# Hybrid recurrence and neighbourhood-attention layer: first attention half in grouped pairs, x a slot earlier, ACT's work on fetched rows in source order, first y rows ahead of w_out

## The chip, the cores and the metric

One core of a Trainium2 chip runs the kernel. The metric is the device time of one execution in microseconds (us); the time of a kernel is the median of its runs. The engines are named as the profile names them: PE (TensorE; PEld is its weight load), DVE (VectorE), ACT (ScalarE), POOL (GpSimd) and SP (SyncE, which here issues the DMAs). Each engine takes its own instructions in order and waits for others by semaphores.

## The reference

One encoder layer on 2048 tokens of width 1024, in float32. The tokens are a grid of 32 rows by 64 columns.

```python
h = layernorm(x) * (1 + scale) + shift            # scale, shift, gate from c @ ada_w + ada_b
q_h, i_h, zf_fw, zf_bw, g_h, q_n, k_n, v_n, g_n = split(h @ w_in)     # nine parts, 1024 columns each
y_hg = hgrn2(q_h, i_h, zf_fw, zf_bw, g_h)         # gated linear recurrence, both directions, 8 heads of 128
o    = neighbourhood_attention(q_n, k_n, v_n, rpb)    # 16 heads of 64
y    = concat([y_hg, o * silu(g_n)]) @ w_out
out  = layernorm(alpha * x + gate * y) * ln_g + ln_b
# attention, for one query at (row r, column c) of one head:
#   keys: 8 grid rows by 16 columns around it, clamped inside the grid
#   s = q . k / 8 + rpb[row offset, column offset];  p = softmax(s);  o = p @ v
```

## The kernel before

[...] The split is a copy on ACT (the high part) and a subtraction on DVE or POOL (the low part). `h`, the normalised and modulated x, is kept as such parts, transposed, in the tiles `h`.

The stages follow one another in time.

1. Startup: half of x is read, normalised and transposed, and the first projections are made.
2. First half of the attention (`first_half`), for tokens 0 to 1023. The 16 heads are eight pairs, one window `w` for each pair. For each pair the attention tile of the first 8 query rows (R = 0) is computed; it has four blocks `j` of 16 columns. What later stages need of q, k, v and g is written to device memory (`nq_d`, `nk_d`, `nv_d`, `ng_d`). In the same windows the other half of x is read, normalised, transposed and split.
3. The recurrence (`hgrn`), both halves.
4. Second half of the attention: for each pair the tiles R = 1, 2, 3, twelve blocks, which need rows of the first half; these are read back ("fetched") into buffers named `bk`, four of them.
5. Output projection with `w_out`, residual, layer norm. `w_out` was split earlier and written to device memory in parts (`wo_d`); `wo_get` reads parts back into the places where `h` was, and `y_raw` reads rows of the branches' outputs (`yq`), which `y_split` splits.

In stages 2 and 4 `weave` lays the attention of one pair (`natten_woven`, a generator) over a dense stream of matmuls: the projections of the next pair (`first_stream`, `natten_stream`) or the output projection (`out_stream`). Whenever `natten_woven` yields a number, the stream is advanced to the same share of its total as the yielded numbers have of `steps`. So PE's order is written out by hand, by the order of the source. In one pair the attention's own work is: `scores` (matmuls against the keys' high parts `KA`, `KB`, L1001, and against the low parts `KL`, L1005), `softmax` on DVE and ACT (L1018 to L1028), `turned` (transposes of the shares on PE, L1050, copied out of the accumulator banks by DVE, L1054, and ACT, L1056), and `sums` (shares times V, L1069). The list `pipe` holds the blocks whose sums are still due. In the second half, blocks come in pairs: both blocks' scores stand together. In the first half, each block stands alone: scores of one block, sums of an older one, a stretch of the stream, transposes, another stretch.

Between these steps stand tasks (`tasks(i)`): loads of V and of bias tables, key copies, splits of Q, gates, and in the first half the 32 slots of `first_half`, four for each pair, with the steps of the second half of x (`rows`, `stats`, `scale`, `piece`) and loads for the gate of the residual (`gate_load`, `gate_sum`).

The order on the other engines is made by a scheduler that simulates the kernel. It lets an instruction move ahead of others; work in `tc.high_priority(offset=PRI)`, such as the softmax and the copies out of banks, goes first. `pinned` (`tc.keep_in_program_order`) puts an instruction behind the one traced just before it on its engine. Accumulators are PSUM banks, eight in all: two for the projections (`pj`), and six that are shared out anew in each stage. In the first half these are two for scores (`sc`), two for transposes (`pt`, those of x included), two for the sums (`po`); in the second half four for scores and transposes together (`sp`), and two for sums.

Names in the prediction: L953 is the exponential of a gate; L923 and L924 copy the two high parts of Q, L938 those of keys; L774 and L800 are splits of weights into high and low parts, of which L801 is the low part; L178 is a step of the statistics of x; L273 is the V projection and L279 its copy out of the bank; L260 the other projections; L910 fetches rows, L1390 is the load in `wo_get`, L1394 the load in `y_raw`, L1420 the copy in `y_split`, L1428 the first matmul of the output projection; L473 and L484 belong to the recurrence.

Of the kernel before, what the change touches and what calls it, by code (L numbers as in the profile page):

```python
# [19 lines left out]
P = 128  # L20
# [17 lines left out]
def body(ctx: ExitStack, tc: tile.TileContext, t):  # L38
# [179 lines left out]
    def h_piece(xs, k, hi, lo, early=False):  # L218
        pt = ps("pt")
# [680 lines left out]
    class Prep:  # L900
# [16 lines left out]

        def q(self, R):
# [4 lines left out]
            act.activation(av[0:64], rv[0:64], AF.Copy)  # L923
            act.activation(bv[64:128], rv[64:128], AF.Copy)  # L924
# [4 lines left out]
        def k(self, i):  # L929
            a, b, src, off = KPIECE[self.half][i]  # L930
            n = (b - a) * GW
            raw = (self.bk[src] if src in self.bk else self.raws["k"][src])[:, off:off + n]
# [3 lines left out]
            for z, x, y in (("KA", top, bot), ("KB", bot, top)):  # L936
                z = keys[z]
                act.activation(z[x, o], raw[x], AF.Copy)  # L938
# [11 lines left out]
        def gate(self, R):  # L950
            raw = self.src("g", R)
            sg = tl("sg")
            act.activation(sg, raw, AF.Exp, scale=-1.0)  # L953
# [141 lines left out]
    def natten_woven(st, nxt, pipe, extra=None, finish=False):  # L1095
# [8 lines left out]
        def tasks(i):  # L1104
            for f, *a in now.get(i, []) + later.get(i, []) + extra.get(i, []):
                f(*a)

        if st.half == 0:
            for i, (R, j) in enumerate(n.order):
                pipe.append([n, R, j, n.scores(R, [j])[0]()])  # L1110
                if len(pipe) > 2:
                    m, r, c, pts = pipe.pop(0)
                    m.sums(r, c, pts)
                yield 1
                turn(pipe, 2)
                yield 1
                tasks(i)
            if finish:
                m, r, c, pts = pipe.pop(0)
                m.sums(r, c, pts)  # L1120
                yield 1
                turn(pipe, 1)
                yield 1
                m, r, c, pts = pipe.pop(0)
                m.sums(r, c, pts)
            return
# [27 lines left out]
    SPS = {"sc": 2, "pt": 2, "po": 2}  # L1154
# [92 lines left out]
    def first_half(raws, feed):  # L1247
# [8 lines left out]
        for j in (0, 1):  # L1256
            st.table("top", j)
# [25 lines left out]
        for m in range(8):  # L1283
            slots[2 + m].append((gate_load, m))
            slots[4 + m].append((gate_sum, m))
        slots[5].append((lower_bounds,))
        for g, i in ((0, 11), (1, 22)):
            slots[i].append((rows, g))
            slots[i + 1].append((stats, g))
            slots[i + 2 - g].append((scale, g, 0))  # L1290
            slots[i + 3 - g].append((scale, g, 1))
            for k in range(KT):
                slots[i + 3 - g + k].append((piece, g, k))
        for u in range(2, 8):
            slots[4 * u - 6].append((bias_pair, u))
        for w in range(8):
# [4 lines left out]
            else:  # L1301
                nxt, dense, total, steps = None, hgrn_dense(0, 0, feed=feed), HTOT, 10
# [45 lines left out]
    with tc.manual_schedule(engines={mybir.EngineType.PE}):  # L1348
        with psum_phase("st", SPS), phase("st", SB_, SMS), tc.manual_schedule(engines={getattr(mybir.EngineType, e) for e in ("PE", "SP", "Activation", "DVE")}):
# [245 lines left out]
```

## Time and profile before

| | |
|---|---|
| time, median of 3 runs | 2683.83 us (2682.41 to 2684.12) |
| the profiled execution | 2687.64 us, span 2685.8 us |
| mean granted clock of PE | 0.989 |
| PE, PEld busy | 2585.7 us (96%), 2154.1 us (80%) |
| DVE, ACT, POOL busy | 66%, 53%, 4% |
| DMA | 313.25 MB, 117 GB/s on average |

The span runs from the first to the last instruction of the profiled execution. Busy time is summed over the instructions of an engine. An idle stretch of an engine is put down to the instruction that released it: "PE pj L273 <- ACT vt L279" is a matmul of line 273, into tile `pj`, that waited for an ACT instruction of line 279 which wrote `vt`. In rows of the timeline, the first number is the start in us from the beginning of the span, the second the duration, `x2` the number of instructions that were joined, and brackets hold the wait before it. In rows of the table of stretches stand the stretch, its length, then for PE, PEld, DVE, ACT and POOL the busy time with the number of instructions, then the granted clock of PE (1.00 is full speed), the busy share of the DMA engines, and GB/s.

### The profile page before, as it was taken

How to read it: one execution, taken by the hardware profiler on the slowest of the kernel's cores; microseconds unless marked ns; L12 is line 12 of the kernel's file. 1: busy time of each engine (PE TensorE's matmuls, PEld its weight loads, DVE VectorE, ACT ScalarE, POOL GpSimd, SP SyncE). 2: the span in 40 equal slices, each digit the busy share in tenths (PEclk: the TensorE clock that was granted, in tenths of full speed). 3: DMA queues.
4: the chain of work that ended last, by engine and by line, in shares of the span. 5: the costliest groups of instructions: out<-in, count | busy, mean ns of one | idle time of the engine just before them, and what ended most of it. 6: DMA issues, size and time to landing. Idle time of an engine off the chain costs nothing.

```text
span 2685.8 us, 46076 instructions
## 1 busy us (share of the span) xinstructions
PE 2585.7 (96%) x17328; PEld 2154.1 (80%) x17328; DVE 1764.1 (66%) x4351; ACT 1423.0 (53%) x2808; POOL 106.6 (4%) x143
## 2 busy tenths in 40 slices
PE   4999999999999999999999999979999998999998
PEld 3888888878888888888888888878877776788887
DVE  5445445478777778877777877545787776548443
ACT  4534444366666666666666666444666665331110
POOL 0000000000000000000000000000000000032221
PEclk8999999999999999999999999999999999999999
DMA  6566454312222237312221122353444446544331
GB/s 235 158 179 161 127 164 150 112 64 91 79 83 87 80 103 242 108 58 75 76 78 61 62 73 83 99 161 98 123 135 130 132 133 175 159 150 134 98 94 55
DMA packets 235777, 313.25 MB, mean 117 GB/s; under 512 B 29480, under 2 KB 118312, under 8 KB 235433
## 3 DMA queue, kind: packets, MB, share of 16 engines
q1 hardware_dynamic: 235553, 310.30, 37.6%
q8 instruction: 136, 2.23, 0.4%
q14 instruction: 88, 0.72, 0.1%
HBM read 226.63 MB, written 75.37 MB: 112 GB/s over the span
## 4 chain that ended last, share of the span: by engine, by line
PE 67%; DMA 4%; DVE 4%; ACT 2%; issue 1%; SPq 1%; DVEq 0%; ACTq 0%
PE pj L260 37%; PE ps L1430 4%; PE ps L1428 4%; PE ps L1429 4%; PE ps L1069 2%; PE ps L1050 2%; PE ps L473 2%; PE pj L273 2%; PE ps L465 1%; PE ps L1001 1%; PE ps L540 1%; PE ps L564 1%; PE ps L566 1%; PE ps L512 1%; DMA bias<-tint 1%; PE ps L1005 1%
## 5 line engine op out<-in xcount | busy, mean ns | idle before, releaser
L260 PE MATMUL pj<-h,wh 128*128 128x512 f32 x4016 | 1283.3, 400 | 12.3 <-ACT h L225 5.9
L260 PEld LDWEIGHTS pj<-h,wh 128*128 128x128 f32 x4016 | 730.0, 189 | 170.6 <-issue 14.8
L260 PE MATMUL pj<-h,wl 128*128 128x512 f32 x2008 | 787.2, 392 | 0.0
L260 PEld LDWEIGHTS pj<-h,wl 128*128 128x128 f32 x2008 | 377.8, 188 | 82.9 <-DVE wl L801 0.4
L273 PE MATMUL pj<-wh,h 128*128 128x256 f32 x1024 | 195.2, 288 | 13.1 <-ACT vt L279 12.8
L1023 ACT ACTIVATE pbuf<-pbuf,mx 128x480 f32<-128x480 f32 (+2 forms) x224 | 143.1, 640 | 121.8 <-DVE mx L1018 120.4
L1018 DVE CUSTOM_DVE_ANT_1 pbuf<-ps,bias 128x480 f32<-128x480 f32 (+2 forms) x224 | 125.7, 590 | 106.2 <-PE ps L1005 91.2
L273 PEld LDWEIGHTS pj<-wh,h 128*128 128x128 f32 x1024 | 163.7, 193 | 16.8 <-ACT vt L279 14.1
L251 DVE TENSOR_TENSOR wl<-wr,wh 128x512 fp32r<-128x512 f32 x192 | 131.7, 686 | 45.6 <-ACT wh L250 44.8
L250 ACT ACTIVATE wh<-wr 128x512 fp32r<-128x512 f32 x192 | 120.2, 626 | 72.9 <-PE pj L260 60.0
L1056 ACT ACTIVATE pt<-ps 128x512 f32<-128x512 f32 (+1 forms) x128 | 69.1, 540 | 148.1 <-PE ps L1050 147.9
L273 PE MATMUL pj<-wl,h 128*128 128x256 f32 x512 | 145.8, 285 | 0.0
L1054 DVE COPY pt<-ps 128x512 f32<-128x512 f32 (+1 forms) x128 | 79.4, 620 | 87.8 <-PE ps L1050 86.9
L1050 PE MATMUL ps<-ident,pbuf 128*128 128x128 f32 x776 | 106.2, 274 | 12.2 <-ACT pt L1056 12.2
L459 DVE TENSOR_TENSOR de<-e,de 128x512 f32<-128x512 f32 x64 | 44.3, 692 | 108.5 <-ACT de L458 108.5
L1050 PEld LDWEIGHTS ps<-ident,pbuf 128*128 128x128 f32 x776 | 92.2, 140 | 28.4 <-ACT pt L1056 13.0
L1404 ACT ACTIVATE yh<-yr 128x512 fp32r<-128x512 f32 x52 | 32.7, 629 | 134.0 <-PE ps L1429 115.4
L1477 DVE TENSOR_TENSOR vt<-ps,gt 128x512 f32<-128x512 f32 x24 | 16.5, 692 | 128.5 <-PE ps L1430 128.5
L1069 PE MATMUL ps<-pt,V 128*64 128x128 f32 x1408 | 100.3, 278 | 0.5 <-DMA V<-nv 0.5
L273 PEld LDWEIGHTS pj<-wl,h 128*128 128x128 f32 x512 | 99.1, 194 | 0.8 <-issue 0.5
L1028 DVE TENSOR_SCALAR pbuf<-pbuf,mx 128x480 f32<-128x480 f32 (+2 forms) x224 | 96.0, 437 | 5.4
L748 ACT ACTIVATE e<-pj 128x512 f32<-128x512 f32 x100 | 59.3, 594 | 74.2 <-PE pj L260 68.6
(271 smaller groups left out, 4722.7 us busy)
## 6 DMA issues: line engine op xcount, KB each, us to landing
wr<-in_w_in SPq DMA_DIRECT2D x276, 256.0 KB
V<-nv SPq DMA_DIRECT2D x256, 64.0 KB
yr<-yq SPq DMA_DIRECT2D x64, 256.0 KB
bias<-tint SPq DMA_DIRECT2D x24, 480.0 KB
x<-in_x SPq DMA_DIRECT2D x32, 256.0 KB
ada<-in_ada_w SPq DMA_DIRECT2D x16, 512.0 KB
wr<-in_w_v SPq DMA_DIRECT2D x32, 256.0 KB
nv<-vt SPq DMA_DIRECT2D x32, 256.0 KB
```

The source lines that it names most:

```text
L250: act.activation(hi, raw, AF.Copy)
L251: dve.tensor_tensor(lo, raw, hi, op=ALU.subtract)
L260: pe.matmul(pz, a, b, start=(k == 0 and n == 0), stop=(k == KT - 1 and n == 2))
L273: pe.matmul(pzs[tp][:, i * 256:(i + 1) * 256], a, b, start=(k == 0 and n == 0 and i == 0), stop=(k == KT - 1 and n == 2), skip_group_check ...
L1018: return dve.tensor_tensor_reduce(s[:, 0:nk].rearrange("p (r c) -> p r c", c=32), sc[:, 0:nk].rearrange("p (r c) -> p r c", c=32), bt[:, 0 ...
L1023: act.activation(s[:, 0:nk], s[:, 0:nk], AF.Exp, scale=-1.0, bias=mx[:, 0:1], accum_out=mx[:, 1:2])
L1028: dve.tensor_scalar(s[:, 0:nk], s[:, 0:nk], mx[:, 2:3], 1.0, op0=ALU.mult, op1=ALU.mult)
L1050: pe.transpose(ptp[:, c * P:(c + 1) * P], s[:, c * P:(c + 1) * P], ident)
L1069: pe.matmul(self.po[R][hs_, j * P:(j + 1) * P], self.st.V[c0 + c][:, j * P + hh * 64:j * P + hh * 64 + 64], pts[hh][:, c * P:(c + 1) * P], ...
L1428: pe.matmul(pz, yh[:, kk], wh, start=first, stop=False)
L1429: pe.matmul(pz, yh[:, kk], wl, start=False, stop=False)
L1430: pe.matmul(pz, yl[:, kk], wh, start=False, stop=last)
```

## The change

1. First half, `natten_woven`: the four blocks of a pair come as two groups of two. The sums that are due stand first, then the scores of both blocks of the group, then both softmaxes; after a stretch of the stream the transposes of both blocks, then another stretch. The tasks of a pair keep their slots; within a slot the `extra` ones come first, in the second half too. The banks are shared out as in the second half (four for scores and transposes), with one for the sums and one for the transposes of x. Three top bias tables are loaded ahead of the first window instead of two, and the last window is counted as 9 steps instead of 10.
2. `first_half`: the loads for the residual's gate and all steps of x stand one slot earlier (the second group's scaling and pieces keep theirs).
3. `Prep`: the ACT instructions that read fetched rows (Q of R = 1, key pieces 0 and 1, gate of R = 1) are pinned to the order of the source.
4. The first four y rows are loaded at slots 2 and 3 of the second half's pair 6, pinned, into buffers of `vt`; before, they were loaded at slots 10 and 11 into weight buffers. For the second column of `w_out`, the first two parts are read ahead of pair 7, and the others one slot earlier than before.

```diff
 def h_piece(xs, k, hi, lo, early=False):
-    pt = ps("pt")
+    pt = ps("hx")
...
 class Prep:
+    def pin(self, raw):
+        return pinned if any(raw is z for z in self.bk.values()) else lambda ins: ins
...  # in q, k and gate:
-        act.activation(av[0:64], rv[0:64], AF.Copy)
-        act.activation(bv[64:128], rv[64:128], AF.Copy)
+        pin = self.pin(raw)
+        pin(act.activation(av[0:64], rv[0:64], AF.Copy))
+        pin(act.activation(bv[64:128], rv[64:128], AF.Copy))
...
-            act.activation(z[x, o], raw[x], AF.Copy)
+            pin(act.activation(z[x, o], raw[x], AF.Copy))
...
-        act.activation(sg, raw, AF.Exp, scale=-1.0)
+        self.pin(raw)(act.activation(sg, raw, AF.Exp, scale=-1.0))
...
 def natten_woven(st, nxt, pipe, extra=None, finish=False):
     def tasks(i):
-        for f, *a in now.get(i, []) + later.get(i, []) + extra.get(i, []):
+        for f, *a in extra.get(i, []) + now.get(i, []) + later.get(i, []):
             f(*a)
     if st.half == 0:
-        for i, (R, j) in enumerate(n.order):
-            pipe.append([n, R, j, n.scores(R, [j])[0]()])
-            if len(pipe) > 2:
-                m, r, c, pts = pipe.pop(0)
-                m.sums(r, c, pts)
-            yield 1
-            turn(pipe, 2)
-            yield 1
-            tasks(i)
-        if finish:
-            ...
+        for i in (0, 2):
+            sums(pipe, 0)
+            for j, soft in zip((i, i + 1), n.scores(0, (i, i + 1))):
+                pipe.append([n, 0, j, soft()])
+            yield 2
+            tasks(i)
+            turn(pipe, 2)
+            turn(pipe, 1)
+            yield 2
+            tasks(i + 1)
+        if finish:
+            sums(pipe, 0)
+            yield 1
         return
...
-    SPS = {"sc": 2, "pt": 2, "po": 2}
+    SPS = ({"sc": 2, "pt": 2, "po": 2}, {"hx": "pt"})
+    NPS0 = ({"sp": 4, "po": 1, "hx": 1}, {"sc": "sp", "pt": "sp"})
...  # first_half
-        for j in (0, 1):
+        for j in (0, 1, 3):
             st.table("top", j)
...
         for m in range(8):
-            slots[2 + m].append((gate_load, m))
-            slots[4 + m].append((gate_sum, m))
+            slots[1 + m].append((gate_load, m))
+            slots[3 + m].append((gate_sum, m))
-        for g, i in ((0, 11), (1, 22)):
+        for g, i in ((0, 10), (1, 21)):
             slots[i].append((rows, g))
             slots[i + 1].append((stats, g))
-            slots[i + 2 - g].append((scale, g, 0))
-            slots[i + 3 - g].append((scale, g, 1))
+            slots[i + 2].append((scale, g, 0))
+            slots[i + 3].append((scale, g, 1))
             for k in range(KT):
-                slots[i + 3 - g + k].append((piece, g, k))
+                slots[i + 3 + k].append((piece, g, k))
...  # the second half's windows
                 if u == 6:
-                    extra = {6: [(wo_get, 0, 0, 1)], 7: [(wo_get, 0, 2)], 8: [(wo_get, 0, 3)], 9: [(wo_get, 0, 4, 5)], 10: [(y_early, 0), (wo_get, 0, 6)], 11: [(y_early, 1), (wo_get, 0, 7)]}
+                    extra = {6: [(wo_get, 0, 0, 1)], 7: [(wo_get, 0, 2)], 8: [(wo_get, 0, 3)], 9: [(wo_get, 0, 4, 5)], 10: [(wo_get, 0, 6)], 11: [(wo_get, 0, 7)]}
+                    for i in (2, 3):
+                        extra[i] = [(lambda tt: y_early(tt, alloc=lambda: tl("wr")), i - 2)]
             else:
                 y_split(0, 1)
                 dense, total = out_stream(list(range(NE))), NE * 16 * KUS
-                extra = {i: [(wo_get, 1, 2 * i, 2 * i + 1)] for i in range(4)}
+                wo_get(1, 0, 1)
+                extra = {i: [(wo_get, 1, 2 * i + 2, 2 * i + 3)] for i in range(3)}
```

More of the change, by code (lines that the diff above doesn't have):

```diff
@@ L931, in k @@
             n = (b - a) * GW
-            raw = (self.bk[src] if src in self.bk else self.raws["k"][src])[:, off:off + n]
+            raw = self.bk[src] if src in self.bk else self.raws["k"][src]
+            pin, raw = self.pin(raw), raw[:, off:off + n]
             o = slice(a * GW, b * GW)
@@ L1104, in tasks @@
         def tasks(i):
-            for f, *a in now.get(i, []) + later.get(i, []) + extra.get(i, []):
+            for f, *a in extra.get(i, []) + now.get(i, []) + later.get(i, []):
                 f(*a)
         if st.half == 0:
-            for i, (R, j) in enumerate(n.order):
-                pipe.append([n, R, j, n.scores(R, [j])[0]()])
-                if len(pipe) > 2:
-                    m, r, c, pts = pipe.pop(0)
-                    m.sums(r, c, pts)
-                yield 1
-                turn(pipe, 2)
-                yield 1
-                tasks(i)
-            if finish:
-                m, r, c, pts = pipe.pop(0)
-                m.sums(r, c, pts)
-                yield 1
[L1122 to L1125, printed above, removed]
+            for i in (0, 2):
[10 more added lines that the diff above has]
+                sums(pipe, 0)
+                yield 1
             return
@@ L1301, in first_half @@
             else:
-                nxt, dense, total, steps = None, hgrn_dense(0, 0, feed=feed), HTOT, 10
+                nxt, dense, total, steps = None, hgrn_dense(0, 0, feed=feed), HTOT, 9
             r = weave(natten_woven(st, nxt, pipe, extra, w == 7), dense, total, steps)[1]
@@ L1348, in body @@
     with tc.manual_schedule(engines={mybir.EngineType.PE}):
-        with psum_phase("st", SPS), phase("st", SB_, SMS), tc.manual_schedule(engines={getattr(mybir.EngineType, e) for e in ("PE", "SP", "Activation", "DVE")}):
+        with psum_phase("st", *SPS), phase("st", SB_, SMS), tc.manual_schedule(engines={getattr(mybir.EngineType, e) for e in ("PE", "SP", "Activation", "DVE")}):
             raws, feed = startup()
-        with psum_phase("n0", SPS), phase("n0", NB0, SM0):
+        with psum_phase("n0", *NPS0), phase("n0", NB0, SM0):
             natten_init(4, 0)
@@ L1390, in wo_get, with y_raw @@
                 pinned(dma(wo[k, n][s].bitcast(F32), wo_d[2 * k + n][s]))
-    def y_raw(tt, q):
-        raw = wp.tile([P, 512], F32, tag="wraw", name=nm("yr"), bufs=WR)
-        dma(raw.rearrange("p (a b) -> p a b", b=P), yq[q][:, :, tt * P:(tt + 1) * P])
+    def y_raw(tt, q, alloc=None):
+        raw = alloc() if alloc else wp.tile([P, 512], F32, tag="wraw", name=nm("yr"), bufs=WR)
+        (pinned if alloc else lambda i: i)(dma(raw.rearrange("p (a b) -> p a b", b=P), yq[q][:, :, tt * P:(tt + 1) * P]))
         return raw
@@ L1408, in body, with y_early @@
     yraws, yhl = {}, {}
-    def y_early(*tts):
+    def y_early(*tts, alloc=None):
         for tt in tts:
             for q in range(2):
-                yraws[tt, q] = y_raw(tt, q)
+                yraws[tt, q] = y_raw(tt, q, alloc)
     def y_split(*tts):
```

## The prediction

> **What bounds the kernel now.** I read the page's busy line first, then the list of waits for PE alone, then the granted clock in stretches, and last the timelines of ACT and SP ahead of the long waits.
>
> ```profile
> span 2685.8 us, 46076 instructions
> PE 2585.7 (96%) x17328; PEld 2154.1 (80%) x17328; DVE 1764.1 (66%) x4351; ACT 1423.0 (53%) x2808; POOL 106.6 (4%) x143
> ```
>
> PE is busy for all but 100 us of the span. So only two things can pay: PE's idle time, and PE's own time for the same matmuls. The waits of PE, longest first after the one at startup:
>
> ```profile
> PE pj L273 <- ACT vt L279: 12.8, 2, 11.9
> PE ps L1050 <- ACT pt L1056: 12.2, 2, 11.2
> PE pj L260 <- ACT h L225: 5.9, 7, 1.4
> PE ps L1001 <- DVE pt L1054: 5.2, 5, 1.0
> PE ps L331 <- DVE rh L326: 4.6, 8, 1.4
> PE ps L473 <- DVE Sf L484: 4.0, 2, 2.8
> PE pj L1428 <- DMA wo<-wod: 3.6, 1, 3.6
> PE pj L260 <- ACT wh L774: 2.9, 1, 2.9
> PE pj L260 <- ACT wh L800: 2.1, 1, 2.1
> ```
>
> Columns: total, times, longest. Two single waits, 11.9 and 11.2 us, stand out. I call them A and B, the 3.6 C, the 2.9 D, the 2.1 E, the 2.8 F. They cost more than themselves, because the clock falls after them (PEclk is the last column but two):
>
> ```profile
> 355.00:394.00 39.00, 39.00 (x270) 33.93 (x268) 15.97 (x41) 15.81 (x34) 0.76 (x3) 1.00 0.52 165
> 296.04:299.45 3.41, 3.41 (x12) 2.24 (x12) 0.53 (x2) 0.00 (x0) 0.00 (x0) 0.50 0.71 235
> 1808.74:1814.96 6.22, 6.22 (x29) 6.22 (x30) 4.32 (x11) 4.29 (x9) 0.00 (x0) 0.50 0.73 233
> 1836.00:2272.00 436.00, 427.12 (x3035) 345.48 (x3033) 335.83 (x961) 283.13 (x633) 6.28 (x20) 1.00 0.50 131
> 2280.51:2286.00 5.49, 5.49 (x19) 3.86 (x19) 5.14 (x16) 4.39 (x10) 0.00 (x0) 0.50 0.45 145
> 2313.31:2316.72 3.41, 3.38 (x9) 1.99 (x9) 0.00 (x0) 0.00 (x0) 0.00 (x0) 0.50 1.05 381
> ```
>
> PE works at 0.50 for 6.22 us after A, 5.49 after B, 3.41 after C and 3.41 after E; half of each stretch is lost.
>
> **Wait A, and the pins.** ACT takes its instructions in order, and the scheduler had put the next pair's gate (L953) far ahead of its place. Rows of the timeline, ACT's and SP's (start, duration, instruction, wait before it):
>
> ```profile
> 1805.78 0.63 ACT L953 ACTIVATE sg<-bk 128x512 f32<-128x512 f32 x1 [18.24 <-DMA bk<-ng]
> ...
> 1808.10 1.07 ACT L279 ACTIVATE vt<-pj 128x512 f32<-128x512 f32 x2
> 1801.93 0.32 SPq L910 DMA_DIRECT2D bk<-ng  x1
> ```
>
> ACT stands for 18.24 us on a row whose load SP issued only at 1801.93. Behind it wait the two copies of `vt` that free PE's accumulators. The pin holds L953 (and Q, K from fetched rows, L923, L924, L938) behind the ACT instruction traced just before it; the gate's place is slot 11, the end of the pair. The same instructions run, none is added. Gain: 11.9 + 6.22/2 = 15.0 us. What is late next: V rows and key copies, which SP issues until 1805, but the blocks that need them come after several more microseconds of projections; I take 0 and keep half of A and B together, 14.5 us, as the rival below.
>
> The four fetched rows' buffers come free later by it, and SP's next fetch with them: 0, since the next fetch is issued when the pair after begins, behind that gate. The pin has another price. Before, the gate, Q and K of the next pair floated into free places. Now the gate's work falls on each pair's end, where five waits of 1.0 (L1001 on DVE's L1054) show DVE to be tight. Queued there are ACT's other copies and DVE's; the gate brings DVE one clamp and one product. The nearest row is that wait itself: between 0 and another 1.0 at seven ends. I take 0.5 each, 3.5 us, because softmax and bank copies have priority over the gate. Below nothing it can hardly be: those waits could vanish if ACT or DVE have less in that place, 5 us at most.
>
> **Wait B, and the first y rows.** Timeline again:
>
> ```profile
> 2264.29 0.63 ACT L924 ACTIVATE Q<-e 64x512 fp32r<-64x512 f32 x1
> 2277.73 0.63 ACT L1420 ACTIVATE yh<-yr 128x512 fp32r<-128x512 f32 x1 [12.81 <-DMA yr<-yq]
> ...
> 2279.98 0.47 ACT L1056 ACTIVATE pt<-ps 128x384 f32<-128x384 f32 x1
> 2267.76 2.01 SPq L1390 DMA_DIRECT2D wo<-wod  x4
> 2269.87 3.76 SPq L1394 DMA_DIRECT2D yr<-yq  x2
> ```
>
> Again ACT's queue has a split of a fetched row (L1420) at its head, for 12.81 us, and the bank copy L1056 behind it. The row's load was issued at 2269.87, behind w_out's parts, which wait on PE for the buffers of h. The change issues the four loads at slots 2 and 3 of pair 6, some 40 us ahead, into buffers of `vt` that nothing uses then. L1420 finds its rows landed. Gain: 11.2 + 5.49/2 = 13.9 us. On SP the four loads move past w_out's parts and into the stream of V rows and weights; four of them took 2.69 us (row below), and SP's own issue is not what PE waits for in pair 6, so 0, at most those 2.7 us.
>
> ```profile
> 2303.13 2.69 SPq L1394 DMA_DIRECT2D yr<-yq  x4
> 2305.91 5.49 SPq L1390 DMA_DIRECT2D wo<-wod  x8
> ```
>
> **Wait C, and w_out's second column.** Its last eight loads were issued from 2305.91 on, just ahead of PE's wait. Now two parts come before pair 7 begins, the others one slot earlier each, and ahead of the key copies of their slot (extra work first). Sixteen issues move past four key copies and eight V loads on SP; these are needed a third of the pair later. Gain 3.6 + 3.41/2 = 5.3 us. But with B gone PE comes to this place 14 us sooner, while SP has the same issues to make: between 5.3 gained and 5.3 lost. I take 5.3 with 1.0 given back, since half of each load's lead is won by order alone.
>
> **First half: grouped pairs.** One step of one block, in PE's timeline:
>
> ```profile
> 251.75 0.32 PE L1001 MATMUL ps<-KA,q 128*128 128x352 f32 x1
> 251.91 0.32 PE L1001 MATMUL ps<-KB,q 128*128 128x352 f32 x1
> 252.17 0.43 PE L1005 MATMUL ps<-KL,q 64*128 64x352 f32 x2
> 252.53 0.88 PE L1069 MATMUL ps<-pt,V 128*64 128x128 f32 x12
> 253.33 0.73 PE L260 MATMUL pj<-h,wh 128*128 128x512 f32 x2
> ```
>
> Starts to starts: 1.58 us, 3.16 for two blocks. The second half already groups:
>
> ```profile
> 1926.92 0.62 PE L1005 MATMUL ps<-KL,Q 64*128 64x384 f32 x4
> 1927.47 0.88 PE L1069 MATMUL ps<-pt,V 128*64 128x128 f32 x12
> ...
> 1929.37 0.73 PE L260 MATMUL pj<-h,wh 128*128 128x512 f32 x2
> ```
>
> Four KL take 0.55 there at 384 columns, so 0.55 x 352/384 = 0.50 here, against 2 x 0.36. All 32 sums take 1.90, and 12 alone 0.80; so 12 more cost (1.90 - 0.80) x 12/20 = 0.66, and 24 take 1.46 against 1.60. KA and KB: 3 x 0.16 + 0.26 = 0.74 against 0.84. Entering the sums straight from projections adds a change of shape, 0.26 - 0.16 = 0.10. Together 0.10 + 1.46 + 0.74 + 0.50 = 2.80; saved 0.36 per group, and 16 groups (two for each of eight pairs) give 5.8 us. The same counts of instructions run on every engine. [...]
>
> The softmax of two blocks must now end within a quarter of a pair. A pair without V took 39 us with 15.97 us of DVE and 15.81 of ACT (first row of the clock stretches): even all DVE work of half a pair, 8 us, is less than the quarter's 9.75. I take 3.0 us for small new waits in 16 groups, bounds 0 and the slower rival. The transposes of x get a bank of their own (one, spaced a slot), the sums one instead of two, read half a pair before its reuse: 0. The third table loaded at the start: 0, behind the V projection of the first pair; the next pair's second table has half a pair of lead instead of three quarters, some 20 us: 0.
>
> **x a slot earlier.** Wait E:
>
> ```profile
> 286.69 0.21 ACT L178 ACTIVATE l<-v 128x4 f32<-128x4 f32 x1 [7.24 <-DVE v L176]
> ```
>
> ACT stands 7.24 us for the statistics of x, then has the scalings, powers and weight splits (L800) all at once, when the V projections end. A slot earlier, eight loads, eight statistics and eight scalings come before and during those projections, where PE asks ACT for little. Gain 2.1 + 3.41/2 = 3.8; if the statistics now meet a softmax, 0, or the same lost. I take 3.8. F lies behind DVE's backlog as the recurrence starts; the sums that end the half come a ninth of the window sooner, so it may go (2.8, and by the stretch after E another 1.7 for the clock); I take 0. D stays: the split L774 keeps its place.
>
> **The sum.** 15.0 + 13.9 + 5.3 + 5.8 + 3.8 = 43.8 gained; 3.5 + 1.0 + 3.0 = 7.5 given back, some of it doubtful; forecast 36.3 less. The profiled execution took 2687.64 us (span 2685.8), 3.8 above the median of 2683.83, so 2651.3 there and 2647.5 as a median. [...]
>
> **Rivals.** (1) Forecast, 0.52. (2) A and B only shrink: ACT or SP has another fetched thing at its head, and half of 28.9 is given back: 2662. For it: SP issues without pause before A and around B. Against: ACT did nothing else for 18 and 13 us. 0.22. (3) Nothing is given back and F goes too: 2683.8 - 43.8 - 4.5 = 2635.5; 0.15. (4) Slower: in each first-half group PE waits for banks or for the second block's softmax, all four score banks being taken at once. It decides from 36.3/16 = 2.3 us a group, with the clock 1.7 lower behind each: at 1.0 + 1.7 it is even worse than the gain, 36.3 - 43 = 7 us slower, 2690.6. The second half runs on such a pool of four: five waits of 1.0 there and no stretch at half clock from 1836 to 2272 (1.00 in the row), so 0.07. [...] (5) No change within 0.2%, 5.4 us, about what a measurement here can tell: the gains of the second half lost again at pair ends, 0.04.
>
> Cases 1 to 3 hold 0.89. The range is 2633 to 2666: from case 3 with a little more to case 2 with C lost. The likeliest case alone: 2640 to 2655.
>
> **What would show it.** Right: L953 no longer among ACT's waits on DMA; L1420 without a wait; PE's L273 and L1050 waits under 2 us each; no half-clock stretch near those places; two KL groups and 24 sums together in the first half. Wrong: L1001 or L1050 waiting on DVE in the first half, pair ends with more than 1.0, or PE waiting for w_out longer than 3.6.

## The result and the profile after

The changed kernel takes 2670.41 us (median of 5 runs, 2663.61 to 2675.12) against 2683.83 before: ratio 0.9949, 95% interval 0.9932 to 0.9966, 13.4 us less. Forecast were 36.3 less and a range from 2633 to 2666. It is faster, by little more than a third of the forecast.

The profiled execution took 2663.61 us, 6.8 below its median, and that of before 3.8 above its own; the two profiles differ by 24.0 us, the medians by 13.4. So places are read from the profiles here, and sizes of whole parts from ratios (0.001 is 2.7 us; the ratio 0.9949 makes 13.7). Line numbers move by the change: after it L1006 and L1010 are the scores, L1023 is the first step of the softmax, L1074 the sums, L1055 the transposes, L1059 and L1061 their copies; L718, L725 and L726 load bias tables, L944 copies keys from one half of the partitions to the other, L952 loads V; L1392 is the load in `wo_get`, L1396 that in `y_raw`, L1422 the copy in `y_split`, L1430 the first matmul of the output projection.

Where the 24.0 lie, from the starts of three rows in each PE timeline: the first scores of the first half's last pair, of the second half, and of pair 6's last group. Before (L1001), then after (L1006, the same instruction):

```profile
486.62 0.41 PE L1001 MATMUL ps<-KA,q 128*128 128x352 f32 x1
1781.92 0.39 PE L1001 MATMUL ps<-KA,Q 128*128 128x480 f32 x1
2260.99 0.34 PE L1001 MATMUL ps<-KA,Q 128*128 128x384 f32 x1
```

```profile
480.18 0.43 PE L1006 MATMUL ps<-KA,q 128*128 128x352 f32 x1
1771.03 0.39 PE L1006 MATMUL ps<-KA,Q 128*128 128x480 f32 x1
2230.16 0.34 PE L1006 MATMUL ps<-KA,Q 128*128 128x384 f32 x1
```

Gained are 6.4 us up to the first half's last pair, 4.5 to the second half, 19.9 in pairs 0 to 6. From pair 6's last scores to the end of the span it is 2685.8 - 2261.0 = 424.8 before and 2661.8 - 2230.2 = 431.6 after: 6.8 lost, where the forecast had 18.2 gained. I call this stretch the tail. The gain ahead of it, 30.8 us in all, is the upper end of what the runs show: in the seven profiles of kernels that differ from the changed one in the tail alone (after_again, y_late, half_wo, late_half, no_table, no_col and table_spread, below), pair 6's last scores start at 2232.8 to 2241.2, which is 20 to 28 us ahead of before. So most of the difference between 24.0 and 13.4 lies ahead of the tail. PE's waits after the change:

```profile
PE ps L1006 <- issue: 13.6, 1, 13.6
...
PE pj L1430 <- DMA wo<-wod: 4.6, 1, 4.6
PE pj L1430 <- ACT yh L1422: 3.6, 2, 2.4
PE pj L260 <- ACT wh L774: 2.9, 1, 2.9
PE pj L273 <- ACT vt L279: 2.5, 1, 2.5
...
PE ps L1055 <- DVE pt L1059: 1.5, 1, 1.5
```

A (11.9 before L273) is down to 2.5, B (11.2 before the transposes) is gone, and so are E and the five waits of 1.04 at pair ends. C is gone too. C was a wait on the second column of `w_out`: in PE's timeline it stands before the 21st matmul of L1428, and the first column, eight parts for two token tiles, has the first 16. The 4.6 us after the change stand before the eighth matmul of L1430 (at 2273.06), so they are a wait on the last part of the first column. In B's place stands a wait of 13.6 before pair 7's scores. What the new wait is, the timelines of SP, DVE and PE and SP's own list of waits tell:

```profile
2229.41 0.72 SPq L725 DMA_DIRECT2D bias<-tedge  x1
2230.18 0.51 SPq L726 DMA_DIRECT2D bias<-tint  x1
...
2231.77 0.60 SPq L718 DMA_DIRECT2D bias<-tint  x1
2232.41 5.03 SPq L1392 DMA_DIRECT2D wo<-wod  x4
2242.36 3.65 SPq L1396 DMA_DIRECT2D yr<-yq  x3
2247.75 0.52 SPq L944 DMA_DIRECT2D KA<-KA  x1
...
2249.65 1.32 SPq L944 DMA_DIRECT2D KA<-KA  x2
...
2242.43 0.56 DVE L1023 CUSTOM_DVE_ANT_1 pbuf<-ps,bias 128x384 f32<-128x384 f32 x1 [5.09 <-DMA wo<-wod]
...
2253.44 0.74 PE L1006 MATMUL ps<-KA,Q 128*128 128x480 f32 x1 [13.59 <-issue]
...
SPq L1396 <- DMA bias<-tint: 4.8, 1, 4.8
```

PE could go on at 2239.9. The keys' copies (L944), which the scores need, were issued only from 2247.75 on, behind w_out's parts and y rows of the third and fourth tile (L1396, not pinned; the scheduler brought them forward into the weight buffers that the first rows no longer use). SP was not busy with issuing all that time: its list of waits says that it stood for 4.8 us, ahead of these y rows, until a bias table had landed. DVE's last softmax of pair 6 went on in the same moment. The profile names a part of `w_out` as what released it, but this instruction reads a bias table and none of `w_out`, so the table is the likelier one.

The granted clock falls here too: it is 0.57 from 2244 to 2260 (0.67 from the wait's end, 2253.44, on) and 0.74 from 2260 to 2280.

### The profile page after: what moved, and what is told of

Read it like the earlier page. It is cut to its first block, busy times and chain, and to the rows that moved or that the text cites. A ratio compares the mean times of both kernels' runs of the same rounds, so it can differ in the third digit from the quotient of the medians.

```text
span 2661.8 us, 46149 instructions
## 1 busy us (share of the span) xinstructions
PE 2574.7 (97%) x17328; PEld 2151.1 (81%) x17328; DVE 1761.2 (66%) x4351; ACT 1417.6 (53%) x2808; POOL 105.3 (4%) x143
## 4 chain that ended last, share of the span: by engine, by line
PE 87%; DVE 5%; DMA 4%; ACT 3%; issue 1%; SPq 0%; DVEq 0%; ACTq 0%
PE pj L260 49%; PE pj L273 5%; PE ps L1431 4%; PE ps L1430 4%; PE ps L1432 4%; PE ps L1074 3%; PE ps L1055 3%; PE ps L473 2%; PE ps L1006 2%; PE ps L465 1%; PE ps L1010 1%; PE ps L540 1%; PE ps L564 1%; PE ps L566 1%; PE ps L512 1%; DMA V<-nv 1%
## 5 line engine op out<-in xcount | busy, mean ns | idle before, releaser
L1023 DVE CUSTOM_DVE_ANT_1 pbuf<-ps,bias 128x480 f32<-128x480 f32 (+2 forms) x224 | 125.5, 589 | 117.5 <-PE ps L1010 95.7
L273 PE MATMUL pj<-wh,h 128*128 128x256 f32 x1024 | 193.6, 287 | 2.8 <-ACT vt L279 2.5
L273 PEld LDWEIGHTS pj<-wh,h 128*128 128x128 f32 x1024 | 162.7, 193 | 6.1 <-ACT vt L279 3.4
L251 DVE TENSOR_TENSOR wl<-wr,wh 128x512 fp32r<-128x512 f32 x192 | 131.5, 685 | 45.7 <-ACT wh L250 44.4
L273 PE MATMUL pj<-wl,h 128*128 128x256 f32 x512 | 145.5, 284 | 0.3 <-DVE wl L801 0.3
L1059 DVE COPY pt<-ps 128x512 f32<-128x512 f32 (+1 forms) x128 | 79.0, 618 | 58.9 <-PE ps L1055 58.1
L1061 ACT ACTIVATE pt<-ps 128x512 f32<-128x512 f32 (+1 forms) x128 | 68.9, 539 | 91.1 <-PE ps L1055 89.9
L1055 PE MATMUL ps<-ident,pbuf 128*128 128x128 f32 x776 | 103.8, 274 | 1.5 <-DVE pt L1059 1.5
L1055 PEld LDWEIGHTS ps<-ident,pbuf 128*128 128x128 f32 x776 | 91.2, 141 | 15.5 <-DVE pt L1059 1.7
L273 PEld LDWEIGHTS pj<-wl,h 128*128 128x128 f32 x512 | 98.8, 193 | 1.3 <-DVE wl L801 0.5
L801 DVE TENSOR_TENSOR wl<-wr,wh 128x512 fp32r<-128x512 f32 x68 | 46.8, 690 | 78.7 <-ACT wh L800 68.2
```

The source lines that it names most:

```text
L251: dve.tensor_tensor(lo, raw, hi, op=ALU.subtract)
L273: pe.matmul(pzs[tp][:, i * 256:(i + 1) * 256], a, b, start=(k == 0 and n == 0 and i == 0), stop=(k == KT - 1 and n == 2), skip_group_check ...
L1023: return dve.tensor_tensor_reduce(s[:, 0:nk].rearrange("p (r c) -> p r c", c=32), sc[:, 0:nk].rearrange("p (r c) -> p r c", c=32), bt[:, 0 ...
L1055: pe.transpose(ptp[:, c * P:(c + 1) * P], s[:, c * P:(c + 1) * P], ident)
```

## The experiments

Ratios are to the kernel before, run beside each kernel. "Wait" is PE's wait before pair 7's scores; "tail" is read as above. The intervals are 0.001 to 0.0017 to either side, so the difference of two rows is uncertain by some 0.002, 5 us. Waits and tails come from one profile each.

| run | ratio (95%) | wait, us | tail, us |
|---|---|---|---|
| kernel before | 1 | none | 424.8 |
| changed kernel | 0.9949 (0.9932 to 0.9966) | 13.6 | 431.6 |
| after_again | 0.9949 (0.9935 to 0.9962) | 15.2 | 432.5 |
| no_pin | 0.9984 (0.9975 to 0.9993) | 1.5 | 427.4 |
| no_group | 0.9983 (0.9973 to 0.9992) | 16.0 | 434.8 |
| no_slot | 0.9979 (0.9970 to 0.9988) | 16.8 | 435.1 |
| no_y | 0.9929 (0.9916 to 0.9941) | 11.7 | 430.6 |
| gate_pin | 0.9946 (0.9931 to 0.9961) | 1.9 | 429.6 |
| before_gate | 0.9964 (0.9951 to 0.9976) | 0.2 | 424.1 |
| y_pinned | 1.0761 (1.0746 to 1.0776) | 10.2 | - |
| y_late | 0.9937 (0.9925 to 0.9949) | 12.5 | 427.5 |
| ord_back | 0.9970 (0.9959 to 0.9982) | 10.2 | 429.8 |
| wo_early | 0.9929 (0.9917 to 0.9941) | 8.3 | 421.9 |
| half_wo | 0.9914 (0.9900 to 0.9928) | 11.1 | 423.1 |
| late_half | 0.9914 (0.9901 to 0.9927) | 8.2 | 419.8 |
| no_table | 0.9915 (0.9901 to 0.9929) | 11.2 | 426.7 |
| mix | 0.9922 (0.9910 to 0.9935) | 5.3 | 423.2 |
| mix_d | 0.9909 (0.9896 to 0.9922) | 9.0 | 420.8 |
| no_col | 0.9900 (0.9885 to 0.9915) | 0.4 | 413.7 |
| table_spread | 0.9937 (0.9923 to 0.9951) | 5.8 | 422.9 |

y_pinned has another last stage, so its tail is not compared. wo_early has a new wait of 3.3 us just ahead of its tail.

**The changed kernel again.**

> The changed kernel once more, to have it beside the next three on one chip and to see how far its own waits move from run to run. Expected: ratio 0.995, the wait before L1006 between 11 and 17 us as in the runs that keep the pins on the keys.

The wait moves by 1.6 us and the time by nothing.

### Each part undone

**no_pin**

```diff
-            return pinned if any(raw is z for z in self.bk.values()) else lambda ins: ins
+            return lambda ins: ins
```

> The changed kernel without the pins on ACT's work on fetched rows. Theory: the pins took away wait A and also the five waits of 1.04 us at the ends of the second half's pairs (both are absent after the change), so both come back: a wait of PE on L279 of about 12 us with the clock at half behind it, 15 us, and 5 us at pair ends; about 2690 us against 2670.4 of the changed kernel. Rival: the place of the gate depended on the old order of the first half and does not return; then no wait over 3 us on L279 and 2670 to 2675.

PE's waits:

```profile
PE pj L1430 <- DMA wo<-wod: 13.0, 2, 8.6
PE pj L273 <- ACT vt L279: 12.2, 3, 10.8
...
PE ps L1006 <- DVE pt L1059: 6.1, 6, 1.0
```

A is back with 10.8 and the waits at pair ends with six of 1.0, as the theory said; the pins are worth 0.0035, 9.4 us, about half of what it had. The wait before pair 7's scores goes, but the last two parts of w_out's first column are waited for 13.0 in its place: the tail shortens by 4 us only.

**no_group** (banks, tables and steps of before too)

```diff
-            for i in (0, 2):   # two blocks' scores together
+            for i, (R, j) in enumerate(n.order):   # one block
```

> The changed kernel with the first half's blocks one by one again (banks, tables and steps of before too). Theory: grouping gained about 6 us of PE's own time (the stretch from the first scores to those of the first half's last pair took 373.5 us before and 367.5 after), so 2676; the wait before L473 where the recurrence starts (2.8 us before, 1.6 after) returns with its half clock, another 3: 2679. Rival: the 6 us come from x's new slot and the wait that went with it (E, 3.8); then grouping is worth 2 us, 2672.

```profile
PE ps L473 <- DVE Sf L484: 2.8, 1, 2.8
```

Ratio 0.9983: grouping is worth 9.1 us with F, which comes back at the recurrence's start as the theory said (after the change 1.6 us are left in that place, behind ACT).

**no_slot**

```diff
-            slots[1 + m].append((gate_load, m))
+            slots[2 + m].append((gate_load, m))
...  # the same for gate_sum and the first group of x; rows and stats of the second
```

> The changed kernel with x and the residual's gate back in their old slots of the first half. Theory: with grouped scores, wait E (2.1 us before L260 on L800, with 3.4 us at half clock) was gone by the slots, so it returns: 4 us slower than the changed kernel, ratio to before about 0.996 to 0.997. Rival: grouping took E away by itself, and the slots are worth nothing: ratio 0.995 as the changed kernel's.

The slots are worth 8.1 us by the ratios, twice the theory's, though with the uncertainty above not surely more than it. E is not at its old place; two others of its kind are there, in PE's timeline:

```profile
169.12 0.38 PE L273 MATMUL pj<-wh,h 128*128 128x256 f32 x1 [1.66 <-ACT wh L800]
...
455.28 0.33 PE L221 MATMUL ps<-ident,x 128*128 128x128 f32 x1 [2.25 <-ACT x L214]
```

**no_y**

```diff
-                    extra = {6: ..., 10: [(wo_get, 0, 6)], 11: [(wo_get, 0, 7)]}
-                    for i in (2, 3): extra[i] = [(lambda tt: y_early(tt, alloc=...), i - 2)]
+                    extra = {6: ..., 10: [(y_early, 0), (wo_get, 0, 6)], 11: [(y_early, 1), (wo_get, 0, 7)]}
...  # pair 7's w_out slots, and the order within a slot of the second half, as before
```

> The changed kernel with the first y rows and w_out's parts back in their old slots and buffers. From the first scores of pair 7's predecessor's last group to the end the profile of before took 415.8 us, that of the changed kernel 422.6, with a new wait of 13.6 us before L1006. Theory: part 4 itself put that wait there, and lost about what wait B had cost: undone, wait B (L1055 on L1061, 11 us) returns and the 13.6 goes; the time is the same or up to 7 us less, 2663 to 2671. Rival: the 13.6 us come from the pins or from the earlier end of the windows before; then undoing part 4 adds its forecast gain, 14 to 19 us, and the time is about 2685.

The time is as the theory said, the reason not: B does not come back, and the 13.6 does not go. With the pins, PE stands before pair 7's scores (11.7) ahead of the place where B was. A wait of 3.5 on the second column is back, as C was. So part 4 as a whole is worth nothing here: without it the ratio is lower by 0.0020, and the intervals only just overlap. The forecast had 18.2 us for it.

**ord_back**, the order within a slot alone:

```diff
-            for f, *a in extra.get(i, []) + now.get(i, []) + later.get(i, []):
+            for f, *a in (now + later + extra if st.half else extra + now + later):   # of slot i
```

> The changed kernel with the order of tasks within a slot of the second half as before (the extra tasks last), so that the bias tables of pair 6 and the key copies of a slot stand ahead of w_out's parts of that slot. Theory: the softmax of pair 6's last block waited until 2242.4 for its table; this wait goes, but the key copies still stand behind the parts of slot 9 and the y rows: ratio 0.992 to 0.995. Rival: the order within the slot is what put the keys late; then the wait before L1006 falls below 5 and the ratio to 0.990.

Both missed: the wait falls to 10.2, and the time rises (2676.8 us against 2671.5 of after_again on the same chip). The order is the same in no_y and in ord_back; they differ in part 4's y rows and in pair 7's w_out slots, and no_y is 0.0041, 11 us, faster. With that order, what part 4 moved costs 11 us. Which of the two moves does it was not tried.

### Which pin

**gate_pin**: in the changed kernel, `pin` stays in `gate` alone. **before_gate**: the kernel before with the gate's `act.activation` pinned and nothing else.

> The changed kernel with only the gate pinned; Q and keys from fetched rows float as before. Theory: the gate alone made wait A, so A stays away (no wait over 3 us on L279); the pins on the keys put pair 7's key copies behind w_out's parts, so the wait of 13.6 us before L1006 goes, but the waits on w_out parts that stood in the run without pins come (8.6 and 4.4 us): ratio 0.994 to 0.996. And the five waits of 1.04 us at pair ends: if they come from the gate's place they stay away, if from the keys' they return (5 us). Rival: A needs the keys pinned too; A returns with 11 us and the ratio is 0.998.

> The kernel before with one edit: the gate from fetched rows pinned. Theory: wait A (11.9 us and 6.2 at half clock, 15 us) and the five waits of 1.04 at pair ends go, 20 us; wait B stays or shrinks, since L1420 keeps its late rows: ratio 0.993. Rival: as in the whole change, the passage to pair 7 takes back what the earlier pairs give: ratio 0.996 to 0.998.

In both, A and the pair-end waits are away. gate_pin came out as its theory said: it is as fast as the whole change, with 9.3 us on the last two parts of w_out's first column instead of the 13.6. So the pins on Q and the keys decide where PE stands at pair 7's start, and not how long it stands in all. PE's waits in before_gate:

```profile
PE pj L1428 <- ACT yh L1420: 7.4, 2, 6.2
...
PE ps L1050 <- DVE pt L1054: 5.1, 1, 5.1
...
PE pj L1428 <- DMA wo<-wod: 3.8, 1, 3.8
PE pj L1429 <- DMA wo<-wod: 3.1, 1, 3.1
```

This one line is worth 0.0036, 9.7 us, on the kernel before, about half of what its theory had and within the rival's range: 5.1 come back at the place of A, and the tail does not get shorter (424.1 against 424.8), though B as such is gone.

### What holds the tail

**y_pinned** pins every `y_raw`; **y_late** only the four loads in `out_stream`.

```diff
-        (pinned if alloc else lambda i: i)(dma(raw...
+        pinned(dma(raw...                                  # y_pinned
+        (pinned if alloc or hold else lambda i: i)(dma(raw...   # y_late; hold=True in out_stream's y_early
```

> The changed kernel with the loads of all y rows pinned to source order, so that the four loads of the third and fourth token tile no longer stand ahead of pair 7's key copies on SP. Theory (order): these four loads held SP from 2242.4 to 2246 and the key copies to 2247.7; PE's wait of 13.6 us before pair 7's scores falls below 8, the time by 6 or more: 2664 or less. Rival (DMA): the key copies wait for the bias table and the w_out parts issued before them, which land only at about 2242; the wait stays above 11 us and the time within 2 us of 2670.

> The changed kernel with only the four loads of the third and fourth token tile pinned to source order (those of the last stage stay free). In the run with all y rows pinned, the wait before pair 7's scores was 10.2 us instead of 13.6, and the key copies were issued on SP at 2247.3, 4.9 us after the last w_out part, behind a bias table's landing. Theory (the order of the y rows is a small part, the w_out parts and the table ahead of the key copies are the large one): wait 10 to 11 us, time 3 to 5 us below the changed kernel, ratio 0.993. Rival (order is all): wait below 3, ratio 0.989.

y_pinned lost 7.6%, for a reason that has nothing to do with the question: it held the loads of the last stage to source order too, and there PE waited 15 times for the split of a row:

```profile
PE ps L1430 <- ACT yh L1406: 171.7, 15, 12.7
```

Its wait before pair 7 (10.2) and y_late's (12.5) say that the y rows' order is a small part, as y_late's theory had it: 1 to 5 us of 13.6 to 15.2. y_late, SP and DVE:

```profile
2241.41 0.72 SPq L725 DMA_DIRECT2D bias<-tedge  x1
2242.18 0.51 SPq L726 DMA_DIRECT2D bias<-tint  x1
...
2254.26 0.52 SPq L944 DMA_DIRECT2D KA<-KA  x1
...
2254.34 0.56 DVE L1023 CUSTOM_DVE_ANT_1 pbuf<-ps,bias 128x384 f32<-128x384 f32 x1 [7.49 <-DMA bias<-tint]
...
SPq L944 <- DMA bias<-tint: 7.0, 2, 4.7
```

The bias table of pair 6's last block landed only 12 us after its issue; the softmax had waited 7.49 us for a table, SP stood before the key copies for one as well, and DVE and the key copies went on together.

**half_wo**, **late_half** (with y_late's edit), **no_col** (with y_late's edit): less of w_out's first column.

```diff
-            for s in range(2):
+            for s in (0,) if n == 0 else (0, 1):    # half_wo, late_half: high parts only
...
+            if n == 0: wo[k, n] = [hts[0, k, s] for s in range(2)]; continue   # no_col: not loaded
```

> The changed kernel, but of w_out's first column only the high parts are loaded (8 loads of 256 KB less around the end of pair 6); the products with the low parts use the high parts in their place, so the output leaves out the low parts of that column. Theory (the loads around pair 6's end are more than the DMA engines pass in that time, so that the key copies, the bias table and the parts land late): the waits from pair 6's last scores to the third quarter of pair 7, 20.6 us, fall below 10, and the ratio to 0.989 or less. Rival (what stands ahead on SP, not bytes): the y rows and the tables are still ahead of the keys, the wait before L1006 stays above 9 and the ratio above 0.992.

> The third and fourth tiles' y rows pinned, and of w_out's first column only the high parts loaded (the output leaves out that column's low parts). With the y rows pinned alone the wait before L1006 was 12.5 us, with half of the column alone 11.1. Theory (bytes): with both, table and key copies share the DMA engines with 2 MB less and land 6 us or more earlier; the wait falls below 6, ratio 0.989. Rival (one transfer that is late for another reason): above 9, ratio 0.991 to 0.993.

> The third and fourth tiles' y rows pinned, and none of w_out's first column loaded: the output projection's first half of columns uses what stands in those buffers, h itself, so the output leaves out that column. Theory (w_out's first column makes the wait): no wait over 3 us before L1006, and the tail from pair 6's last scores falls from 418 (with the column) to about 398; ratio 0.985. Rival (tables, V rows and keys would do it alone): a wait over 6 us stays, ratio 0.989 or more.

half_wo alone missed its theory: the wait stays at 11.1, as the rival had it, and the ratio is 0.9914. With the y rows away the wait goes with the loads of this column: 12.5 (y_late), 8.2 (late_half, between its theory and its rival), 0.4 (no_col, as its theory said). These kernels take bytes off the DMA engines and issues off SP together; what speaks for the landings is SP's list of waits above, where SP stands until tables have landed. The stretches that begin 2 to 3 us after pair 6's last scores, in the changed kernel (scores at 2230.16) and then in no_col (at 2241.21):

```profile
2232.00:2244.00 12.00, 7.84 (x61) 6.32 (x57) 6.85 (x22) 4.81 (x12) 0.00 (x0) 1.00 0.93 171
```

```profile
2244.00:2257.83 13.83, 10.27 (x76) 7.75 (x73) 11.38 (x36) 11.00 (x26) 0.00 (x0) 1.00 0.45 123
```

The DMA share is 0.93 against 0.45; PE is idle for the last 4 of 12 us in the first and for 3.6 of 13.8 in the second, there mostly for the y split. Still the tail is 413.7, not the 407 that the theory had (398 to the last matmul and 9 behind it), and the ratio 0.9900 and not 0.985: 3.2 before the y splits and 2.0 for the second column remain.

**no_table** (y_late's edit, pair 6's last table not loaded) and **table_spread** (y_late's edit, the table in eight DMAs):

```diff
+            key = kind, JT[1 if (kind == "bot" and j == 3 and self.p == 6) else j]      # no_table
...
-            dma(bf[0:64, 4 * 64:12 * 64], table_ap(tedge[p], 15, jt, 4, 0, 8))
+            for i in range(4):                                                          # table_spread
+                dma(bf[i * 16:i * 16 + 16, 4 * 64:12 * 64], part_ap(tedge[p], 15, jt, i, 0, 8))
...  # the same for rows 64 to 127
```

> The third and fourth tiles' y rows pinned, and pair 6's last bias table not loaded: its last block uses the table of the block before, so the output leaves out that table. In the run with the y rows pinned alone, the table was issued at 2241.4 and 2242.2 and DVE's last softmax and SP's key copies both went on at 2254.3. Theory (the late table is the cause): both go on 8 us or more earlier; the wait before L1006 falls below 5, ratio 0.989. Rival (the parts of w_out as such): the key copies are issued behind them all the same, wait above 9, ratio 0.992 to 0.994.

> The third and fourth tiles' y rows pinned, and pair 6's last bias table loaded by eight DMAs of 16 partitions instead of two of 64 (same bytes, same places). In the run without this edit the table was issued at 2241.4 and 2242.2 and DVE's last softmax went on at 2254.3, 12 us later, after 7.5 us of wait. Theory (a load of 64 partitions by 4 strides runs on few DMA engines and queues there): in sixteens it lands within 8 us and DVE's wait falls below 3.5; the wait before L1006 stays near 11, since the key copies have other tables ahead of them. [...] Rival (all sixteen engines are full): the landing stays at 11 to 13 us and the time is the same or some us longer by the six more issues on SP.

Without the table the keys wait 11.2 all the same, so no_table's theory missed: other tables are ahead of them. With it in sixteens, SP and DVE:

```profile
2235.55 2.08 SPq L731 DMA_DIRECT2D bias<-tedge  x4
2237.67 2.68 SPq L733 DMA_DIRECT2D bias<-tint  x4
...
2244.11 0.55 DVE L1033 CUSTOM_DVE_ANT_1 pbuf<-ps,bias 128x384 f32<-128x384 f32 x1
```

The softmax runs 3.8 us after the last issue, without a wait (7.5 in y_late), and the wait before the scores is 5.8, better than the theory had it; the tail is 4.6 shorter. Part of this is a head start: measured from pair 6's last scores, the table's first issue is 3.4 us earlier than in y_late. In the ratio nothing of it is seen (0.9937 both).

**wo_early** (y_late's edit, first column at slots 6 and 7), **mix**, **mix_d**: other orders.

```diff
+ extra = {6: [(wo_get, 0, 0, 1, 2, 3)], 7: [(wo_get, 0, 4, 5, 6, 7)]}     # wo_early, mix_d
+ extra = {6: [(wo_get, 0, 0, 1, 2)], 7: [(wo_get, 0, 3, 4)], 8: [(wo_get, 0, 5, 6, 7)]}   # mix
  # mix and mix_d: pin in gate alone, y_late's edit, extra tasks last in a slot
```

> As the run before it, and the loads of w_out's first column all at slots 6 and 7 of pair 6, ahead of the key copies by two thirds of a pair instead of around them. Theory: the key copies of pair 7 then stand behind no w_out part that is still under way; the wait of 10 to 14 us before L1006 falls below 3 and the waits on w_out parts stay under 5: ratio about 0.988, 2652 us. Rival (DMA's throughput is the bound of this stretch, whatever the order): the wait moves to w_out's second column or to pair 6, and the ratio stays within 0.002 of the changed kernel's 0.995.

> The changed kernel with four things together: only the gate pinned, the third and fourth tiles' y rows pinned, tasks within a slot in the old order, and w_out's first column at slots 6 (parts 0 to 2), 7 (3, 4) and 8 (5 to 7). Theory (order on SP decides which wait ends last): tables and key copies are ahead, the parts are all issued before pair 7; waits around pair 7's start below 8 us together, ratio 0.988. Rival (throughput): the sum of the waits there stays at 14 to 20 us in other places, ratio 0.992 to 0.995.

> As the run of four things together, but w_out's first column at slots 6 (parts 0 to 3) and 7 (4 to 7), each behind the bias table of its slot, so that the last table and the key copies have no part of w_out issued between them. There the waits were 5.3 before the scores, 3.4 and 1.8 behind, ratio 0.9922. Theory: the table lands sooner and the wait before L1006 falls below 3, ratio 0.990. Rival (the same bytes in the same time): no change, 0.992.

None of these orders brings the wait under 5 us, so on the waits all three theories missed: mix has 5.3 before the scores and 3.4 and 1.8 behind, wo_early 8.3 and a new one of 3.3 in pair 6. The ratios of wo_early and mix come nearer their rivals, that of mix_d nearer its theory. mix_d, PE:

```profile
PE ps L1006 <- issue: 9.0, 1, 9.0
...
PE pj L1430 <- ACT yh L1422: 4.3, 2, 3.1
```

Its wait on w_out's parts is gone, and at 0.9909 it is the fastest of those that leave nothing out: 24 us less than before, against 13.7 for the change. So here the order counts beside the number of loads.

## Why the prediction was wrong

**Wait B and wait C: the step that failed.** The prediction took 13.9 + 5.3 - 1.0 here and wrote that the loads moved past others on SP cost "0, at most those 2.7 us", and that what sixteen parts of `w_out` move past is "needed a third of the pair later". B and C themselves went, as it said. The term for what stands behind them, which it put at nothing, was wrong: a wait of 13.6 before pair 7's scores and one of 4.6 on the first column of `w_out` came in their place, with the clock down behind both (0.67 from 2253.44 to 2260, 0.50 for 3.41 us from 2273.06 on). The tail lost 6.8 us (7.7 in after_again) instead of gaining 18.2, and with part 4 undone the kernel is no slower. The prediction asked what ACT's L1420 waits for and took what stood behind it as free.

The runs show that at pair 6's end more loads are due than land in that time: with one load first, another is late (keys 13.6, or w_out's parts 13.0, or the y split 6.2), and only without the loads of the first column do these waits nearly all go. Order and form of the loads are worth a part of it (tails of 420.8 and 422.9 in mix_d and table_spread). How much is bytes, form or order is not shown. The prediction's second rival named this kind ("ACT or SP has another fetched thing at its head") and had half of A and B, 14.5 us, given back; the tail is 25 us behind the forecast, and A stayed gone. The prediction's own sign of being wrong, PE waiting for `w_out` longer than 3.6, is there with 4.6.

What should have been read beside the names of the waits is the DMA share. It was there to read in before, in the rows around B and C (the first one is of SP, with no engine's busy time):

```profile
2205.00:2280.00 75.00, 0.95 0.64 168
2260.00:2280.00 20.00, 9.31 (x70) 7.26 (x68) 6.50 (x19) 6.40 (x15) 0.00 (x0) 0.81 0.83 226
```

The long row hides with 0.64 what the short one shows with 0.83, and the prediction's own row behind C has 1.05: there was little free time for a load to move into.

**Wait A: right in kind.** 2.5 is left of 11.9, a little above the 2 that the prediction named as the sign of being right, and a stretch of 3.41 us at 0.50 is left behind it. The gate's pin alone does it (gate_pin, before_gate). All pins together are worth 9.4 us by the ratios, where the forecast had 15.0 - 3.5.

**The pins' price: wrong sign.** Taken were 3.5 us lost at pair ends. The waits of 1.04 vanished instead, and come back without the pins: they came from the gate that floated (before_gate pins nothing else, and they are gone). The changed kernel, from 1850 to 2230:

```profile
1850.00:2230.00 380.00, 379.69 (x2705) 306.84 (x2704) 306.28 (x885) 254.10 (x579) 5.49 (x18) 1.00 0.50 138
```

**Grouping: right, a little low.** One group in PE's timeline after the change:

```profile
240.52 1.53 PE L1074 MATMUL ps<-pt,V 128*64 128x128 f32 x24
241.98 0.43 PE L1006 MATMUL ps<-KA,q 128*128 128x352 f32 x1
...
242.83 0.59 PE L1010 MATMUL ps<-KL,q 64*128 64x352 f32 x4
243.35 0.50 PE L260 MATMUL pj<-h,wh 128*128 128x512 f32 x1
```

2.83 us from sums to projections, forecast 2.80; that makes 16 x 0.33 = 5.3. No wait of over 0.5 us follows between 135 us and the recurrence, where 3.0 were taken off. F fell from 2.8 to 1.6, which the prediction had at 0. By undoing it, the part is worth 9.1.

**x a slot earlier: perhaps low.** 3.8 forecast, 8.1 by undoing it, each such number uncertain by 5. The undone parts do not simply add (9.4 + 9.1 + 8.1 gained, and 13.7 in all): the wait before pair 7 is longer in no_group and no_slot (16.0, 16.8) too.

So ahead of the tail the forecast was 18.1 (15.0 + 5.8 + 3.8 - 3.5 - 3.0) and the profiles show 20 to 31; in the tail it was 18.2 gained and they show 6.8 and 7.7 lost. That the first sum comes near is in part luck: the pins gave 9.4 where A's term alone had 15.0, and the 6.5 us given back for pair ends and small new waits were not lost. What is still open: how the 8 to 9 us that even mix_d and late_half keep are shared between tables, V rows and keys.

## What to carry to other kernels

A wait that names one late load is not priced by its length until the load next behind it has been looked up: ask for the DMA share of that short stretch first, and where it is near 1 (here 0.83 around B, 0.93 after the change), add up what all the loads of that stretch need, and not the waits. An instruction that a scheduler lets float to the head of an engine's queue can cost twice, as the gate did here: 11.9 us where it stood, and 1.0 at each of five pair ends. Pinning that single one did the work of pinning all (2.5 and 0.5 left of these waits in gate_pin, a ratio of 0.9946 against 0.9949). A load's form is worth a run beside its bytes: here the same table in pieces of sixteen partitions landed within 3.8 us of its last issue instead of 11.7, in part by the earlier issue, though the time of the kernel did not show it (0.9937 both).

## What the hardware showed that was not expected

**A low DMA share while V rows move.** y_late, two stretches: while mostly V rows move, and while tables and w_out's parts share the way:

```profile
2238.00:2243.50 5.50, 5.50 (x52) 4.21 (x50) 4.34 (x12) 4.55 (x10) 0.00 (x0) 1.00 0.30 90
2244.00:2253.00 9.00, 5.33 (x30) 4.18 (x28) 2.82 (x9) 1.43 (x5) 0.00 (x0) 1.00 1.03 180
```

In the first stretch SP issued V rows up to 2241.3, five in 5.18 us, then the table, and the DMA share was 0.30; by estimate that is as much as some five of the sixteen engines busy all the time (0.30 x 16). How many engines a load ran on, no row here shows; that the table, as one load of 64 partitions, ran on few was the author's theory. table_spread fits it: in pieces of sixteen partitions the table came within 3.8 us of its last issue instead of 11.7, part of which is the earlier issue. But the pieces are also smaller and eight instead of two, and no run tells these apart. That V rows and tables queue behind each other, no row shows either; V loads in sixteens were not tried. A share near 1 is also not one speed here: 1.03 goes with 180 GB/s in this second stretch, and 1.05 went with 381 GB/s in the prediction's row behind C.

**The clock after short gaps.** The changed kernel after its waits of 2.94 (L774) and 2.50 (L273), then the kernel before after the same wait on L774:

```profile
1808.55:1811.96 3.41, 3.36 (x14) 2.45 (x15) 1.33 (x3) 0.47 (x1) 0.00 (x0) 1.00 0.43 139
1759.48:1762.89 3.41, 3.41 (x19) 3.41 (x18) 1.90 (x4) 2.62 (x5) 0.00 (x0) 0.50 0.54 148
```

```profile
1832.03:1835.44 3.41, 2.99 (x7) 2.32 (x8) 1.72 (x4) 0.89 (x2) 0.00 (x0) 0.50 0.31 98
```

Behind the same 2.94 us the clock was 0.50 once and 1.00 once, and behind 2.50 it was 0.50. It was 0.50 for 3.41 us behind E's 2.1 as well (the prediction's row at 296.04), and in the changed kernel behind the 4.60 before L1430 (2273.06 to 2276.47). So in these five places the length of a wait alone does not tell whether the clock falls behind it; what does, is not shown.
